# A hybrid decoder step: the state space scan in two halves, and one-operation softmax statistics

## The chip, the cores and the metric

The kernel runs on one core of a Trainium2 chip. The metric is the device time of one launch in microseconds (us); lower is better. The engines are PE (TensorE, matrix products), PEld (its weight loads), DVE (VectorE), ACT (ScalarE), POOL (GpSimd) and SP (SyncE, which here issues transfers). Each has its own instruction stream and runs it in order; semaphores tie the streams together.

## The reference

The program is one layer of a decoder with two branches, for 1024 prompt tokens and 64 new tokens (8 requests of 8). One projection of the normalised input gives the columns of both branches and of all gates. The S5 branch is a linear state space model: 64 groups of 16 channels, each with 64 complex states. The attention branch uses a compressed latent; the new tokens also attend to a paged cache of 4096 past tokens. Cut to what matters here:

```python
z = rmsnorm(x) @ w_in
u_s, g_s, cq, ckv_raw, kr_raw, g_a, m_s, m_a = split_in(z)
# S5 branch, by group g, state p, channel c
bu = einsum('gpc,blgc->blgp', b_bar, ug);  bu[:, 0] += lam_bar * h0
h  = associative_scan(lambda e1, e2: (e1[0]*e2[0], e2[0]*e1[1] + e2[1]), (lam_bar, bu), axis=1)
y  = real(einsum('gcp,blgp->blgc', c, h)) + d * u
y_s = (glu(gelu(y)) * silu(g_s)) @ w_br_ssm
# attention branch: prompt blocks of 128 queries, and pages with running max and sum
m_new = maximum(m, max(sp));  corr = exp(m - m_new);  pp = exp(sp - m_new)
l = l * corr + sum(pp);       acc = acc * corr + pp @ kc
y_a = (o * silu(g_a)) @ w_br_attn
h = x + (sigmoid(m_s) * y_s + sigmoid(m_a) * y_a) @ w_out;  y = rmsnorm(h)
```

## The kernel before

**Stripes.** A projection is computed in stripes of 128 output columns. For one stripe of the input projection PE runs 72 matmuls of 368 or 352 token columns (L152): each product is taken with a high and a low part of both factors. The 128x1024 weights of a stripe come in by SP (`wraw`), ACT casts them to `whi` (L94), and DVE or POOL subtracts to get `wlo` (L100). The stripes are called u, gs, ga, ms, ma by their columns; there are 8 of each.

**The S5 branch** works on blocks of 8 time steps. A *quarter* q is 16 groups, and has two halves h of 8 groups, so each u stripe feeds one half. For each half:

- `s5_inputs` builds the input matrices `Bm` on DVE (L545 to L547, 128x1024), turns them on PE (L553), multiplies them with u, which has been through memory (L561), and ACT copies the result into the state tile `S` (L566).
- `s5_consts` and `s5_toeplitz` build, on POOL, the output matrices `E` (L647 to L649, 128x1152) and the diagonal `dg` (L651), and on PE and ACT the matrix `Km` of the 8 steps in a block (L671 to L683).
- `s5_outputs` gathers the states into `Hg` (L693 on ACT, L694 on POOL), multiplies `Km` with u and `E` with `Hg` (L703, L705), and writes `Y` to memory.

`s5_scan` runs on DVE once for a quarter. The 136 block states are 16 runs of 8 and 8 new-token states. It has three parts: seven rounds of four 256-element operations that run along j, the position in a run (L586 to L589, stride of 8 elements in `S`); 16 steps of four 16-element operations that carry the run ends from run to run in a tile `R`; and a back substitution in 448-element operations (L616 to L619).

**Order.** Python generators issue work, and `woven` picks, at each turn, the stream with the least progress, so the weights of the streams set the order; `urgent`, `pin` and `PLAN` do the same for later stages:

```python
t = min(todo)
d = next(t[2])
t[0] += d / t[3]
...
for q in range(NQ):
    yield from self.woven((chain(q), 40), (self.s5_scan(q, sb), W3))
```

All eight u stripes come first, beside the S5 setup. Then `self.run((self.s5(sb, ps), 256), (fill(), W2))` weaves the S5 work with `fill`, which is 8 ms and 3 gs stripes. After it stand one gs stripe and one ga stripe, then the latents (q, k, v), the prompt attention and the decode attention. Both attentions are woven with "dense" stripes (the other gates, the output projections) by the numbers in `PLAN`, a list of (stripes, from, to) by attention steps. The names that the prediction uses are these: scan (L586 to L622), inputs (L545 to L566), consts (L647 to L651), outputs (L693 to L705), and the softmax lines L1007, L1014 (prompt), L1253, L1254, L1261 (decode).

Of the kernel before, what the change touches and what calls it, by code (L numbers as in the profile page):

```python
# [57 lines left out]
PLAN = ((6, MQ, MP - 1), (6, MP - 1, MP - 1), (3, MP + 2, MP + 14), (40, MP + 14, MD - 20), (2, MD - 18, MD - 1),  # L58
# [17 lines left out]
class Body:  # L76
# [211 lines left out]
    def stage_u(self, raws, outs, sb, ps):  # L288
        yield from self.stripes(self.a["w_in"], C_U, KT, (self.xh, self.xl), KT, raws, outs, ps, self.u_each(sb),
                                first=2)  # L290


    def s5_setup(self, sp, sb, ps):
# [93 lines left out]
        L4 = sp.tile([P, 4, G], F32, name="L4")  # L387
# [8 lines left out]
        tt = sp.tile([P, 2, G], F32, name="tt")  # L396
# [31 lines left out]
        sgn = sp.tile([P, 2], F32, name="sgn")  # L428
# [87 lines left out]
    def s5_inputs(self, q, sb, ps):  # L516

        nc = self.nc
        V = nc.vector
        S = sb.tile([P, PQ, 2, NCK + 1], F32, name="S", bufs=2)  # L520
        self.pin(V.memset(S[:, :, :, 0:1], 0.0), q == 0)
        self.S[q] = S
        for h in range(2):
            while self.u_done < 2 * q + h + 1:
                yield 0.5
            g0 = q * 2 * GB + h * GB
            gs = slice(g0, g0 + GB)
# [4 lines left out]
            U = sb.tile([P, GB, NCK], F32, name="UA")  # L532
# [4 lines left out]
            tb = sb.tile([P, GB, 8, GC], F32, name="tb")  # L537
# [31 lines left out]

    def s5_scan(self, q, sb):  # L570
# [35 lines left out]
        yield 0.8
        w1 = sb.tile([P, PQ // 2, NSUP, 7], F32, name="w1")
        w2 = sb.tile([P, PQ // 2, NSUP, 7], F32, name="w2")
        for a in (slice(0, PQ // 2), slice(PQ // 2, PQ)):
# [15 lines left out]
    def s5_consts(self, q, h, sb, ps):  # L625

        nc = self.nc
        Gp = nc.gpsimd
# [5 lines left out]
        for i in (nc.sync.dma_start(cb, self.bc_dram[0:2, :, gs].rearrange("i p g c -> p i g c")),
                  nc.sync.dma_start(Bz[:, :, GC:2 * GC], self.bc_dram[2, :, gs]),
                  nc.sync.dma_start(U, self.u_dram[:, gs])):
            if q == 0:
                self.behind(i, self.u_last)
# [16 lines left out]

    def s5_toeplitz(self, q, h, sb, ps):

        nc = self.nc
# [5 lines left out]
        for n in range(2):  # L664
            cols = slice(n * P, n * P + P)
            for x in range(3):
                for r in range(4):
                    g = 2 * r + n
                    o = b[r * W:(r + 1) * W, cols]
                    if x == 0:  # L670
                        i = nc.tensor.matmul(o, Bz[:, g, GC:], E[:, g, 1:9].rearrange("p t c -> p (t c)"), start=True, stop=False)  # L671
                        self.pin(i, r == 0)
                    elif x == 1:
                        nc.tensor.matmul(o, Bz[:, g, 0:W], E[:, g, 0:8].rearrange("p t c -> p (t c)"),
                                         start=False, stop=False)
# [1038 lines left out]
```

## Time and profile before

| | |
|---|---|
| median of 3 runs | 1879.74 us (1874.36 to 1880.57) |
| the profiled execution | 1876.06 us, span 1874.3 us, mean granted clock 0.972 |
| PE busy | 1726.3 us (92%) |
| DVE busy | 1232.0 us (66%) |
| ACT busy | 931.1 us (50%) |
| POOL busy | 784.5 us (42%) |

The page of the profile gives the busy time of each engine, and the span in 40 slices of 47 us. By the stages of the program the span reads: input and u stripes until 132 us; the S5 region from 132 to 406 us; one gs and one ga stripe until 430 us; latents until 755 us; prompt attention until 1200 us; decode attention until 1660 us; the last projections until 1874 us. In the slices, PE is at 9 tenths nearly everywhere, but at 6 to 8 tenths in slices 1 to 3 and in slices 4 to 8, the S5 region, where DVE is busiest.

### The profile page before, as it was taken

To read this page: it belongs to the slowest core of one execution; us is meant where nothing else is said; L and a number is where in the kernel's file an instruction comes from. 1 tells how busy PE (TensorE), PEld (TensorE's weight loads), DVE (VectorE), ACT (ScalarE), POOL (GpSimd) and SP (SyncE) were. 2 spreads that over 40 slices of the span, in tenths; PEclk is the share of its full clock that TensorE was granted. 3 is DMA by queue.
4 is the path that set the end of the run, shared out by engine and by line. 5 is a ranking of instruction groups with operands and counts; after the bars stand their busy time and mean duration, and the time that the engine had idled before them with its cause. 6 is when DMAs were issued, how large, how long until landed. Compare 5 with 4: busy or idle time off the path is not lost.

```text
span 1874.3 us, 32546 instructions
## 1 busy us (share of the span) xinstructions
PE 1726.3 (92%) x11434; PEld 1635.8 (87%) x11434; DVE 1232.0 (66%) x2847; ACT 931.1 (50%) x2269; POOL 784.5 (42%) x757
## 2 busy tenths in 40 slices
PE   6998866699998999999999899988999999999997
PEld 6998866699998988999999889887898899899997
DVE  7708999953334442788877888568787787644322
ACT  5226344432346443677766666455566566532222
POOL 2116334403455112665654545555455455322223
PEclk9999988899999999999999999999999999999999
DMA  8444334244456999565655753465555455275602
GB/s 204 139 99 141 103 92 114 53 129 126 122 172 211 326 311 295 132 183 156 188 146 146 202 138 87 153 232 182 177 179 177 162 164 178 85 248 147 192 9 96
DMA packets 263194, 299.60 MB, mean 160 GB/s; under 512 B 40272, under 2 KB 223288, under 8 KB 256760
## 3 DMA queue, kind: packets, MB, share of 16 engines
q1 hardware_dynamic: 234424, 231.97, 42.4%
q0 software_dynamic: 7872, 48.24, 7.5%
q10 hardware_dynamic: 20736, 17.31, 3.4%
q8 instruction: 91, 1.49, 0.3%
q14 instruction: 71, 0.58, 0.1%
HBM read 201.79 MB, written 95.66 MB: 159 GB/s over the span
## 4 chain that ended last, share of the span: by engine, by line
PE 59%; DVE 20%; DMA 9%; ACT 5%; issue 4%; POOL 2%; SPq 1%; ACTq 0%; POOLq 0%; DVEq 0%
PE mm L152 28%; PE sc L152 5%; PE sc L1000 4%; PE acc L1145 4%; PE tr L152 3%; PE tr L1035 3%; DVE sc L586 2%; DVE sc L588 2%; DVE S L589 2%; DMA ck<-cache_ckv,pidx 2%; DVE sc L587 2%; PE sc L1119 1%; PE acc L1049 1%; PE sc L1208 1%; PE acc L1048 1%
## 5 line engine op out<-in xcount | busy, mean ns | idle before, releaser
L152 PE MATMUL mm<-xT,whi 128*128 128x368 f32 (+1 forms) x1920 | 509.0, 339 | 14.2 <-DVE gst L775 13.8
L152 PEld LDWEIGHTS mm<-xT,whi 128*128 128x128 f32 x1920 | 346.0, 193 | 18.7 <-DVE gst L775 14.4
L152 PE MATMUL mm<-xT,wlo 128*128 128x368 f32 (+1 forms) x960 | 321.9, 336 | 0.0
L100 POOL TENSOR_TENSOR cl<-ck,ch 128x1024 fp32r<-128x1024 f32 x64 | 154.9, 2423 | 170.2 <-ACT ch L94 165.5
L152 PEld LDWEIGHTS mm<-xT,wlo 128*128 128x128 f32 x960 | 184.5, 192 | 1.3
L1016 POOL TENSOR_SCALAR p<-p,sm 128x1024 f32<-128x1024 f32 (+7 forms) x128 | 97.8, 768 | 123.4 <-DVE sm L1015 66.3
L94 ACT CAST pTh<-tr 128x256 fp32r<-128x256 f32 (+1 forms) x248 | 110.2, 451 | 68.4 <-PE tr L1035 53.3
L100 DVE TENSOR_TENSOR pTl<-tr,pTh 128x256 fp32r<-128x256 f32 (+1 forms) x248 | 125.9, 511 | 27.6 <-ACT pTh L94 18.2
L1000 PE MATMUL sc<-K,Q 128*128 128x384 f32 (+5 forms) x576 | 133.7, 347 | 5.9 <-ACT p L1011 5.8
L100 POOL TENSOR_TENSOR wlo<-wraw,whi 128x1024 fp32r<-128x1024 f32 x35 | 86.7, 2477 | 112.3 <-ACT whi L94 110.3
L1011 ACT ACTIVATE p<-sc,sm 128x320 f32<-128x320 f32 (+3 forms) x192 | 110.4, 581 | 35.8 <-DVE sm L1008 29.2
L1035 PE MATMUL tr<-ident,p 128*128 128x128 f32 x576 | 112.1, 275 | 9.9 <-DVE pTl L100 7.3
L1004 DVE TENSOR_REDUCE sm<-sc 128x1 f32<-128x128 f32 (+2 forms) x192 | 104.0, 550 | 12.3 <-PE sc L1000 8.4
L1000 PEld LDWEIGHTS sc<-K,Q 128*128 128x128 f32 x576 | 98.6, 191 | 12.8 <-ACT p L1011 8.4
L152 PE MATMUL mm<-z,whi 128*128 128x368 f32 (+1 forms) x384 | 108.2, 346 | 0.0
L152 PE MATMUL mm<-aT,whi 128*128 128x368 f32 (+1 forms) x384 | 107.7, 339 | 0.0
L94 ACT CAST whi<-wraw 128x1024 fp32r<-128x1024 f32 (+1 forms) x74 | 71.4, 965 | 69.9 <-PE mm L152 63.7
L152 PE MATMUL mm<-oT,whi 128*128 128x368 f32 (+1 forms) x384 | 95.3, 330 | 2.7 <-DVE gl L1409 2.7
L1035 PEld LDWEIGHTS tr<-ident,p 128*128 128x128 f32 x576 | 72.3, 141 | 18.6 <-issue 4.5
L1049 PE MATMUL acc<-pTl,Vt 128*128 128x256 f32 (+1 forms) x224 | 82.2, 367 | 1.3 <-DVE pTl L100 1.3
L94 ACT CAST ch<-ck 128x1024 fp32r<-128x1024 f32 x64 | 67.2, 1051 | 25.7 <-DMA ck<-cache_ckv,pidx 20.0
L1048 PE MATMUL acc<-pTh,Vt 128*128 128x256 f32 (+1 forms) x224 | 73.0, 326 | 2.2 <-DVE oT L1054 1.6
(486 smaller groups left out, 4746.4 us busy)
## 6 DMA issues: line engine op xcount, KB each, us to landing
wraw<-w_in SPq DMA_DIRECT2D x45, 512.0 KB, 5.0
krT<-kr_dram SPq DMA_DIRECT2D x64, 192.0 KB, 2.8
kr_dram<-krx SPq DMA_DIRECT2D x64, 128.0 KB, 2.6
v_dram<-vt SPq DMA_DIRECT2D x32, 256.0 KB, 4.3
Q<-qn_dram SPq DMA_DIRECT2D x32, 256.0 KB, 5.2
K<-kn_dram SPq DMA_DIRECT2D x32, 256.0 KB, 5.0
Vt<-v_dram SPq DMA_DIRECT2D x8, 1024.0 KB, 5.7
u_dram<-ust ACTq DMA_DIRECT2D x64, 68.0 KB, 3.6
```

What stands on the lines that cost most here:

```text
L94: nc.scalar.copy(hi, src)
L100: e.tensor_sub(lo, src, hi.bitcast(F32))
L152: i = nc.tensor.matmul(ps, row(s, k)[:, wsl], row(m, k)[(slice(None),) + xsl], start=start and k == j == 0, stop=stop and k == nk - 1 and ...
L586: V.tensor_mul(u1, src, qb(Q, k, n, True))
L1000: self.mark(nc.tensor.matmul(s[:, :w], qq[:, i * P:(i + 1) * P], kk[:, k0:k0 + w], start=j == 0, stop=j == 2), j == 0)
L1004: V.reduce_max(sm[:, x:x + 1], s[:, :w], axis=AX.X)
L1011: nc.scalar.activation(p[:, k0:k0 + w], s[:, :w], AF.Exp, bias=sm[:, 2:3], scale=SCALE, accum_out=sm[:, 3 + x:4 + x])
L1016: nc.gpsimd.tensor_scalar(p[:, :n], p[:, :n], sm[:, 5:6], 0.0, op0=ALU.mult, op1=ALU.add)
L1035: self.mark(nc.tensor.transpose(b[:, x * P:(x + 1) * P], ptl[x][:, k * P:(k + 1) * P], self.ident), x == s0)
L1048: self.mark(nc.tensor.matmul(po[:, o0:], w, th[:, o0:], start=k == 0, stop=False))
L1049: nc.tensor.matmul(po[:, o0:], w, tl[:, o0:], start=False, stop=k == nk - 1)
L1145: self.mark(nc.tensor.matmul(o[:, :KV], t[:kp, i * P:(i + 1) * P], pv(i)[x], start=j == 0 and i == 0, stop=j == 2 and i == nt - 1), i == 0)
```

## The change

The scan works on two halves of 32 groups (four *octets* of 8 groups each) where it worked on four quarters. The state tile is now `W[P, 16, 2, 9, 17]`: position in a run (9) outside and run (17) inside, so that an operation along j reads 16 neighbouring elements. The run carries stand in `W[..., 0, :]` and have no tile of their own. The rounds have 512 elements, the carry steps 32, the back substitution 420 in four pieces of 4 pairs. ACT's copies into `W` now scatter (read along k, write along j), and all four `Hg` copies are on ACT, reading `W` at a stride of 17 elements. `E`, `tm` and `dg` are built on DVE, and `wlo` stays on DVE in this region; both were POOL's.

The front of the program does six of the u stripes (0 to 5); stripes 6 and 7 begin `fill`, followed by 8 ms stripes and one gs stripe. The remaining gs stripes are woven with the outputs of the second half. Two ga stripes come before the latents (was one); `PLAN` has 37 stripes in its fourth entry (was 40), `NGA` is 3 (was 2).

In the softmax, maximum and scaling are one `tensor_scalar` (prompt: max then multiply; decode: multiply then min with the earlier negative maximum), and the two sums are `tensor_scalar`, too. `L4`, `tt` and `sgn` are moved to a scratch pool. The line numbers in the second half of each difference below are those of the new kernel; there, L100 is L102 and L152 is L154.

On POOL, at the place where the first outputs of the scan are made, the instructions before are these (names: `Hg` the gathered states, `E`, `tm`, `dg` and `wlo` as above):

```order
L694 TENSOR_SCALAR Hg<-S 64x4x136 x2
L647 TENSOR_TENSOR E_1412<-Pr,cb 128x8x144
L694 TENSOR_SCALAR Hg<-S 64x4x136 x2
L649 TENSOR_TENSOR E_1412<-E_1412,tm 128x8x144
L648 TENSOR_TENSOR tm<-Pi,cb 128x1152
L100 TENSOR_TENSOR wlo<-wraw,whi 128x1024
L647 TENSOR_TENSOR E_1413<-Pr,cb 128x8x144
L651 TENSOR_TENSOR dg<-dT,ident 32x256
```

Now POOL passes from the clearing of the S5 tiles straight to the gathering of the cached rope keys (`dkr`), which belongs to the stage after:

```order
L479 DMA bc_dram<-By 128x1024
L721 MEMSET Km_1224 128x1024
L722 MEMSET E_1226 128x8x16
L723 MEMSET Bz_1228 128x384
L721 MEMSET Km_1225 128x1024
L722 MEMSET E_1227 128x8x16
L723 MEMSET Bz_1229 128x384
L1177 DMA dkr<-cache_krope,pidx 128x256 x2
```

All of POOL's tensor work of the S5 region is gone from it.

On DVE, in a scan before, the carry steps have only the inputs of the next quarter (`Bm`) between them:

```order
L586 TENSOR_TENSOR sc_2090<-R,Q 128x16
L587 TENSOR_TENSOR sc_2091<-R,QS 128x16
L588 TENSOR_TENSOR sc_2090<-sc_2090,S 128x16
L589 TENSOR_TENSOR R<-sc_2090,sc_2091 128x16
L545 TENSOR_TENSOR Bm<-Pr,cbB 128x1024
L586 TENSOR_TENSOR sc_2090<-R,Q 128x16
```

Now DVE's stream holds consts and `wlo` as well. Here is the end of the first scan's back substitution (`w`), with the `E` of the third octet, which uses the tile of the first, and the first round of the second scan behind it:

```order
L622 TENSOR_TENSOR w_2261<-W,Q 128x420
L648 TENSOR_TENSOR E_1226<-Pr,cb 128x8x144
L624 TENSOR_TENSOR w_2261<-w_2261,w_2262 128x420
L102 TENSOR_TENSOR wlo<-wraw,whi 128x1024
L650 TENSOR_TENSOR E_1226<-E_1226,tm 128x8x144
L625 TENSOR_TENSOR W<-W,w_2261 128x4x7x15
L590 TENSOR_TENSOR sc_2313<-W,QS 128x512
```

What moved is that the second scan stands on DVE behind an `E` whose tile PE must first have read out. The core of the difference:

```diff
-PQ = GB
+OCT = 4
+PQ = OCT * PB
 NSUP = 16
-NGS = 3
-NGB, NGA = 1, 2
+NRUN = NSUP + 1
+NU = 6
+NGB, NGA = 2, 3
...
-PLAN = ((6, MQ, MP - 1), (6, MP - 1, MP - 1), (3, MP + 2, MP + 14), (40, MP + 14, MD - 20), (2, MD - 18, MD - 1),
+PLAN = ((6, MQ, MP - 1), (6, MP - 1, MP - 1), (3, MP + 2, MP + 14), (37, MP + 14, MD - 20), (2, MD - 18, MD - 1),
...
-        S = sb.tile([P, PQ, 2, NCK + 1], F32, name="S", bufs=2)
-        self.pin(V.memset(S[:, :, :, 0:1], 0.0), q == 0)
-        self.S[q] = S
-        for h in range(2):
...
+        W = sb.tile([P, PQ, 2, 9, NRUN], F32, name="W", bufs=2)
+        self.pin(V.memset(W[:, :, :, 0, 0:1], 0.0), q == 0)
+        self.W[q] = W
+        for o in range(OCT):
...
+            while self.u_done <= q * OCT + o:
+                yield 0.2
...
-                        nc.scalar.copy(S[e * 64:(e + 1) * 64, h * PB + n, x, 1:],
-                                       b[x * 64:(x + 1) * 64, e * NCK:(e + 1) * NCK])
+                        nc.scalar.copy(W[e * 64:(e + 1) * 64, o * PB + n, x, 1:9],
+                                       b[x * 64:(x + 1) * 64, e * NCK:(e + 1) * NCK].rearrange("p (k j) -> p j k", j=8))
...
-        for j in range(1, 8):
-            cmac(SPv[:, :, :, :, j], SPv[:, :, :, :, j - 1], SPv[:, :, :, :, j], 0, NSUP, t1, t2)
-            yield 1.0
-        R = sb.tile([P, PQ, 2, NSUP + 1], F32, name="R")
-        V.memset(R[:, :, :, 0:1], 0.0)
+        for j in range(2, 9):
+            cmac(W[:, :, :, j, 0:NSUP], W[:, :, :, j - 1, 0:NSUP], W[:, :, :, j, 0:NSUP], 0, NSUP)
+            yield 2.7
         for k in range(NSUP):
-            cmac(R[:, :, :, k + 1:k + 2], R[:, :, :, k:k + 1], SPv[:, :, :, k, 7:8], 7, 1, t1[:, :, :, 0:1], t2[:, :, :, 0:1])
+            dst = W[:, :, :, 0, k + 1:k + 2]
+            if k == NSUP - 1:
+                dst = self.hfin[:, :, 8, prs].rearrange("p x n -> p n x").unsqueeze(3)
+            cmac(dst, W[:, :, :, 0, k:k + 1], W[:, :, :, 8, k:k + 1], 7, 1)
...
+        n = PQ // 4
...
-                V.tensor_add(SPv[:, a, x, :, 0:7], SPv[:, a, x, :, 0:7], w1)
-                yield 1.5
-        V.tensor_copy(SPv[:, :, :, :, 7], R[:, :, :, 1:NSUP + 1])
-        V.tensor_copy(S[:, :, :, SEQ // 8:NCK], h0)
-        yield 1.0
...
+                V.tensor_add(W[:, a, x, 1:8, 1:NSUP], W[:, a, x, 1:8, 1:NSUP], w1)
+                yield 2.4
...
-        Gp.tensor_mul(E[:, :, 1:10], bp(self.Pr), bc(cb[:, 0]))
-        Gp.tensor_mul(tm, bp(self.Pi), bc(cb[:, 1]))
-        Gp.tensor_add(E[:, :, 1:10], E[:, :, 1:10], tm)
+        V.tensor_mul(E[:, :, 1:10], bp(self.Pr), bc(cb[:, 0]))
+        V.tensor_mul(tm, bp(self.Pi), bc(cb[:, 1]))
+        V.tensor_add(E[:, :, 1:10], E[:, :, 1:10], tm)
...
+        Hg = sb.tile([P, GB, NCK], F32, name="Hg", tag="Bm")
+        Hv = Hg.rearrange("p (n two) (k j) -> p n two k j", two=2, j=8)
         for x in range(2):
-            nc.scalar.copy(Hv[x * 64:(x + 1) * 64, :, 0], S[0:64, h * PB:(h + 1) * PB, x, 0:NCK])
-            nc.gpsimd.tensor_scalar(Hv[x * 64:(x + 1) * 64, :, 1], S[64:128, h * PB:(h + 1) * PB, x, 0:NCK],
-                                    1.0, 0.0, op0=ALU.mult, op1=ALU.add)
-        yield 2.0
-
-        Y = sb.tile([P, GB, NCK], F32, name="Y")
+            for e in range(2):
+                src = W[e * 64:(e + 1) * 64, o * PB:(o + 1) * PB, x, 0:8].rearrange("p n j k -> p n k j")
+                dst = Hv[x * 64:(x + 1) * 64, :, e]
+                nc.scalar.copy(dst, src)
...
+        self.W, self.U = {}, {}
         yield from self.s5_inputs(0, sb, ps)
-        for q in range(NQ):
-            yield from self.woven((chain(q), 40), (self.s5_scan(q, sb), W3))
-        yield from chain(NQ)
+        yield from self.woven((self.s5_scan(0, sb), 53), (self.s5_inputs(1, sb, ps), 22))
+        yield from self.woven((self.s5_scan(1, sb), 53), (self.s5_outs(0, sb, ps), 36))
+
+    def s5_outs(self, q, sb, ps):
+        for o in range(OCT):
+            yield from self.s5_consts(q, o, sb, ps)
+            yield from self.s5_toeplitz(q, o, sb, ps)
+            if o > 0:
+                yield from self.s5_outputs(q, o - 1, sb, ps)
+        yield from self.s5_outputs(q, OCT - 1, sb, ps)
...
-                V.tensor_max(sm[:, 0:1], sm[:, 0:1], sm[:, 1:2])
-            V.tensor_scalar(sm[:, 2:3], sm[:, 0:1], -SCALE, None, op0=ALU.mult)
+                V.tensor_scalar(sm[:, 2:3], sm[:, 0:1], sm[:, 1:2], -SCALE, op0=ALU.max, op1=ALU.mult)
+            else:
+                V.tensor_scalar(sm[:, 2:3], sm[:, 0:1], -SCALE, None, op0=ALU.mult)
...
             if len(parts) == 2:
-                V.tensor_add(sm[:, 3:4], sm[:, 3:4], sm[:, 4:5])
+                V.tensor_scalar(sm[:, 3:4], sm[:, 3:4], sm[:, 4:5], None, op0=ALU.add)
...
             if g >= 0:
-                V.tensor_max(nm[:, 0:1], nm[:, 0:1], d["m"])
-            V.tensor_scalar(nm[:, 1:2], nm[:, 0:1], -SCALE, None, op0=ALU.mult)
+                V.tensor_scalar(nm[:, 1:2], nm[:, 0:1], -SCALE, d["nm"], op0=ALU.mult, op1=ALU.min)
+            else:
+                V.tensor_scalar(nm[:, 1:2], nm[:, 0:1], -SCALE, None, op0=ALU.mult)
...
-                nc.scalar.activation(nm[:, 2:3], d["m"], AF.Exp, bias=nm[:, 1:2], scale=SCALE)
-                V.scalar_tensor_tensor(l, l, nm[:, 2:3], nm[:, 3:4], op0=ALU.mult, op1=ALU.add)
-            d["m"] = nm[:, 0:1]
+                nc.scalar.activation(nm[:, 2:3], d["nm"], AF.Exp, bias=nm[:, 1:2], scale=-1.0)
+                V.tensor_scalar(l, l, nm[:, 2:3], nm[:, 3:4], op0=ALU.mult, op1=ALU.add)
+            d["nm"] = nm[:, 1:2]
...
-                self.wlo = "pool"
 
                 def fill():
+                    yield from self.stage_u(wr, wo, gsb, ps, NU, KT)
                     yield from self.stage_gates(("ms",), wr, wo, gsb, ps)
-                    yield from self.stage_gates(("gs",), wr, wo, gsb, ps, n=NGS)
-                self.run((self.s5(sb, ps), 256), (fill(), W2))
+                    yield from self.stage_gates(("gs",), wr, wo, gsb, ps, n=1)
+                self.run((self.s5(sb, ps), 185), (fill(), 119))
+                self.run((self.s5_outs(1, sb, ps), 36),
+                         (self.stage_gates(("gs",), wr, wo, gsb, ps, first=1, n=4, pin=True), 33))
                 self.s5_states(sb, ps)
-                self.wlo = "dve"
-                self.run((self.stage_gates(("gs",), wr, wo, gsb, ps, first=NGS, n=4, pin=True), 1))
-                self.run((self.stage_gates(("ga",), wr, wo, gsb, ps, n=NGB, pin=True), 1))
+            self.run((self.stage_gates(("ga",), wr, wo, gsb, ps, n=NGB, pin=True), 1))
```

## Rows read from the trace of the kernel before

**Rows 1.** Busy time by stretch: us, PE, PEld, DVE, ACT, POOL busy, granted clock, DMA, GB/s
```profile
135.00:405.00 270.00, 209.91 (x1611) 200.28 (x1609) 247.86 (x509) 123.27 (x360) 113.89 (x56) 0.90 0.38 103
...
755.00:1200.00 445.00, 429.86 (x2699) 403.54 (x2698) 356.91 (x1050) 295.10 (x813) 242.25 (x301) 0.99 0.55 149
1200.00:1660.00 460.00, 433.30 (x2893) 396.86 (x2892) 338.82 (x638) 263.08 (x532) 220.48 (x126) 0.98 0.55 179
```

**Rows 2.** PE's waits, 135 to 405 us: total us, times, longest us
```profile
PE sc L553 <- DVE sc L588: 17.5, 2, 9.3
PE mm L152 <- DVE gst L775: 13.8, 3, 11.4
...
PE sc L703 <- ACT Km L683: 1.3, 1, 1.3
PE tr L705 <- ACT Hg L693: 0.4, 1, 0.4
```

**Rows 3.** Chain of waits in order of time: start us, us, what
```profile
80.82 51.10 PE mm L152 x311
...
406.21 15.87 PE mm L152 x96
```

**Rows 4.** DVE by line and shape, 130 to 405 us: busy us, mean ns | idle
```profile
L589 DVE TENSOR_TENSOR S<-sc,sc 128x256 f32<-128x256 f32 x28 | 33.7, 1205 | 0.7
...
L587 DVE TENSOR_TENSOR sc<-S,QS 128x256 f32<-128x256 f32 x28 | 27.0, 965 | 0.0
```

**Rows 5.** DVE timeline: start us, us, instruction
```profile
198.11 0.19 DVE L586 TENSOR_TENSOR sc<-R,Q 128x16 f32<-128x16 f32 x1
...
198.78 0.19 DVE L586 TENSOR_TENSOR sc<-R,Q 128x16 f32<-128x16 f32 x1
...
227.58 0.62 DVE L619 TENSOR_TENSOR S<-S,w 128x448 f32<-128x448 f32 x1
228.12 0.65 DVE L586 TENSOR_TENSOR sc<-S,Q 128x256 f32<-128x256 f32 x1
...
240.17 3.61 DVE L588 TENSOR_TENSOR sc<-sc,S 128x256 f32<-128x256 f32 x1
...
246.41 0.61 DVE L586 TENSOR_TENSOR sc<-S,Q 128x256 f32<-128x256 f32 x1
...
248.75 0.61 DVE L586 TENSOR_TENSOR sc<-S,Q 128x256 f32<-128x256 f32 x1
```

**Rows 6.** POOL timeline of the same place
```profile
240.63 2.67 POOL L649 TENSOR_TENSOR E<-E,tm 128x1152 f32<-128x1152 f32 x1
```

**Rows 7.** DVE by line and shape, whole run
```profile
L100 DVE TENSOR_TENSOR wlo<-wraw,whi 128x1024 fp32r<-128x1024 f32 x29 | 36.7, 1265 | 29.2 <-ACT whi L94 29.0
L100 DVE TENSOR_TENSOR pTl<-sc,pTh 128x512 fp32r<-128x512 f32 x40 | 27.3, 683 | 9.8 <-ACT pTh L94 9.0 <-PE acc L1145 0.9
```

**Rows 8.** PE timeline near the end of the scan
```profile
282.42 0.40 PE L703 MATMUL sc<-U,Km 128*128 128x136 f32 x2
282.65 0.40 PE L705 MATMUL sc<-Hg,E 128*128 128x136 f32 x2
...
294.46 0.42 PE L671 MATMUL sc<-E,Bz 128*32 128x128 f32 x8
...
296.00 0.66 PE L553 MATMUL tr<-ident,Bm 128*128 128x128 f32 x4
```

**Rows 9.** ACT by line and shape, whole run
```profile
L566 ACT COPY S<-sc 64x136 f32<-64x136 f32 x76 | 20.3, 267 | 6.3 <-PE sc L561 5.3
L772 ACT ACTIVATE gst<-mm 128x368 f32<-128x368 f32 x32 | 15.4, 480 | 14.8 <-PE mm L152 8.0 <-DMA u_dram<-ust 3.9 <-issue 2.7
...
L279 ACT COPY ust<-mm 128x368 f32<-128x368 f32 x16 | 13.8, 886 | 42.5 <-DMA u_dram<-ust 17.6 <-PE mm L152 13.3 <-issue 7.7
L693 ACT COPY Hg<-S 64x544 f32<-64x544 f32 x16 | 10.4, 650 | 29.7 <-DVE S L622 18.8 <-DVE S L619 5.8 <-DMA y_dram<-Y 5.0
```

**Rows 10.** Lines of the decode softmax: ns of one, min/median/max, start us
```profile
L1253 DVE TENSOR_TENSOR dnm<-dnm x64: 140/156/2795, 1234.1 to 1628.7; 128x1 f32<-128x1 f32 x64
...
L1254 DVE TENSOR_SCALAR dnm<-dnm x72: 135/153/155, 1233.5 to 1628.9; 128x1 f32<-128x1 f32 x72
```

**Rows 11.** PE's waits, 1200 to 1660 us
```profile
PE acc L1145 <- DVE dacc L1279: 6.3, 3, 4.9
...
PE tr L1208 <- DVE dnm L1254: 2.4, 3, 0.9
```

More of the change, by code (lines that the diff above doesn't have):

```diff
@@ L286, in u_each, with stage_u @@
         return each
-    def stage_u(self, raws, outs, sb, ps):
-        yield from self.stripes(self.a["w_in"], C_U, KT, (self.xh, self.xl), KT, raws, outs, ps, self.u_each(sb),
-                                first=2)
+    def stage_u(self, raws, outs, sb, ps, first, n):
+        yield from self.stripes(self.a["w_in"], C_U, n, (self.xh, self.xl), KT, raws, outs, ps, self.u_each(sb),
+                                first=first)
     def s5_setup(self, sp, sb, ps):
@@ L386, in s5_setup @@
             self.pin(i, q == 0)
-        L4 = sp.tile([P, 4, G], F32, name="L4")
+        L4 = sb.tile([P, 4, G], F32, name="L4", bufs=1)
         V.tensor_copy(L4.rearrange("p q g -> p (q g)"), b[:, :4 * G])
@@ L395, in s5_setup @@
         V.tensor_copy(Pi[:, 1], L4[:, 1])
-        tt = sp.tile([P, 2, G], F32, name="tt")
+        tt = sb.tile([P, 2, G], F32, name="tt", bufs=1)
         def cmul(dr, di, ar, ai, br, bi, n):
@@ L426, in s5_setup @@
         self.Q, self.QS = Q, QS
-        sgn = sp.tile([P, 2], F32, name="sgn")
+        sgn = sb.tile([P, 2], F32, name="sgn", bufs=1)
         nc.gpsimd.memset(sgn[0:64, 0:1], 1.0)
@@ L531, in s5_inputs @@
                 self.behind(i, self.u_last)
[L532 removed]
+            while self.u_done <= q * OCT + o:
+                yield 0.2
+            U = sb.tile([P, GB, NCK], F32, name="UA", tag="U", bufs=2)
             i = nc.sync.dma_start(U, self.u_dram[:, gs])
@@ L536, in s5_inputs @@
             Bm = sb.tile([P, GB, 8, GC], F32, name="Bm")
-            tb = sb.tile([P, GB, 8, GC], F32, name="tb")
+            tb = sb.tile([P, GB, 8, GC], F32, name="tb", tag="tm")
             def bp(t):
@@ L605, in s5_scan @@
             V.tensor_copy(self.hfin[:, x, 0:8, prs].rearrange("p b n -> p n b"), smp[:, :, x])
[L606 to L609, printed above, removed]
+        V.tensor_copy(W[:, :, :, 0:8, NSUP], h0)
+        yield 3.0
+        n = PQ // 4
+        for a in range(0, PQ, n):
+            a = slice(a, a + n)
+            w1 = sb.tile([P, n, 7, NSUP - 1], F32, name="w1", tag="sc1")
+            w2 = sb.tile([P, n, 7, NSUP - 1], F32, name="w2", tag="sc2")
@@ L618, in s5_scan, with s5_consts @@
                 V.tensor_add(w1, w1, w2)
-                V.tensor_add(SPv[:, a, x, :, 0:7], SPv[:, a, x, :, 0:7], w1)
-                yield 1.5
-        V.tensor_copy(SPv[:, :, :, :, 7], R[:, :, :, 1:NSUP + 1])
-        V.tensor_copy(S[:, :, :, SEQ // 8:NCK], h0)
-        yield 1.0
-    def s5_consts(self, q, h, sb, ps):
+                V.tensor_add(W[:, a, x, 1:8, 1:NSUP], W[:, a, x, 1:8, 1:NSUP], w1)
+                yield 2.4
+    def s5_consts(self, q, o, sb, ps):
         nc = self.nc
-        Gp = nc.gpsimd
-        g0 = q * 2 * GB + h * GB
+        V = nc.vector
+        g0 = (q * OCT + o) * GB
         gs = slice(g0, g0 + GB)
-        cb = sb.tile([P, 2, GB, GC], F32, name="cb")
-        E, Bz, Km = self.Es[h], self.Bz[h], self.Kms[h]
+        cb = sb.tile([P, 2, GB, GC], F32, name="cb", bufs=2)
+        E, Bz = self.Es[o % 2], self.Bz[o % 2]
         U = sb.tile([P, GB, NCK], F32, name="U", bufs=2)
[L634 to L638, printed above, removed]
+        nc.sync.dma_start(cb, self.bc_dram[0:2, :, gs].rearrange("i p g c -> p i g c"))
+        nc.sync.dma_start(Bz[:, :, GC:2 * GC], self.bc_dram[2, :, gs])
+        nc.sync.dma_start(U, self.u_dram[:, gs])
         tm = sb.tile([P, GB, 9, GC], F32, name="tm")
@@ L1539, in front @@
                         yield from self.stage_x(xT, wr, wo, gsb, self.pool(s3, "xs", 2, side=R), ps)
-                    yield from self.stage_u(wr, wo, gsb, ps)
+                    yield from self.stage_u(wr, wo, gsb, ps, 2, NU)
                 with ExitStack() as s3:
```

83 lines of the change are left out of this document (33 added, 50 removed).

## The prediction

> **What bounds the kernel now.** I read the span by stages first, then for each stage what PE waits for, then the engine that PE waits for. In the two attention stages PE is busy 429.86 of 445 us and 433.30 of 460 us [rows 1]: work taken off DVE there can give back at most the remainders, 15 and 27 us. The S5 region differs. In 270 us PE is busy 209.91, at a granted clock of 0.90, while DVE is busy 247.86 [rows 1]. Ten lines of PE's waits, from 17.5 us on DVE's L588 to 0.4 us on ACT's `Hg`, add up to 59 us [rows 2]. DVE sets the pace there.
>
> What that costs follows from PE's own work. 311 stripe matmuls take 51.10 us, 0.1643 us each, so a stripe of 72 is 11.83 us [rows 3]. The S5 products come at 0.116 us each (two pairs of them start at 282.42 and 282.65), and one set of E products takes 1.54 us (294.46 to 296.00) [rows 8]. The region has 384 of the first, 44.5 us; eight sets at some 1.4 us, 11; and the transposes, 8: in sum 63.5 us. When the S5 work is over, at 406.21, the chain has a run of 96 stripe matmuls [rows 3], of which the first 72 are the last gs stripe, which thus ends at 418. From the end of u at 132 us until then there are 12 stripes, 142 us. With the 63.5 us PE could be done at 337.5; the trace has 418, so the region loses 80.5 us. No edit to it can return more.
>
> Why is DVE so slow? A round of four 256-element operations starts at 246.41 and the next at 248.75: 2.34 us, 0.585 each [rows 5]. Yet the means of L589 and L587 are 1205 and 965 ns [rows 4]. The DVE operation that starts at 240.17 takes 3.61 us and ends at 243.78 [rows 5]; POOL's E operation lasts from 240.63 to 243.30 [rows 6]. So a DVE operation with both inputs in SBUF lasts as long as POOL's where they overlap. The 112 operations of the rounds use 121 us, by these means; at 0.585 they would use 65.5.
>
> **The change part by part.**
>
> *DVE in the S5 region.* Removed: the stretching by POOL, whose order is empty there. Rounds: 56 operations of 512 elements. A 512-element DVE subtraction with one input in PSUM takes 683 ns, a 1024-element one from SBUF 1265 [rows 7], half of which is 0.63. I take 0.68: 38 us. Bounds are 0.62 and, if the slowness is not POOL's, twice the present means, 1.93 to 2.41 (a rival, below). Carry: 32 steps instead of 64, of 32 elements; a step of 16 takes 0.67 (198.11 to 198.78) [rows 5], I take 0.73: 23.5 us. Back substitution: 64 operations of 420 elements, where one of 448 starts 0.54 before the next [rows 5]: 34.6. Inputs, 24 at 1.27 [rows 7]: 30.5. Added from POOL: 24 E operations of 1152 elements at 1.40 (the 1265 ns by size), 33.6; `dg`, 8 at some 0.43, 3.4; `wlo`, 14 at 1.27, 17.8. Gate evictions and the rest: 12. In sum 194 us, against 247.86 now, although 55 us of it were POOL's.
>
> *The scan's new layout.* The rounds read 16 neighbours where they read at 32 bytes. The price of the stride on DVE is small or none by the rows: the strided 256 elements take 0.61 when not stretched, the 448 in runs of seven 0.62 [rows 5], so up to 0.25 us of an operation may be the stride's. The 0.68 holds half of that.
>
> *When the scan can start and end.* Six u stripes end at 37.5 + 71 = 108.5 us instead of 132 (37.5 is 132 less eight stripes). In PE's order the products of the first half's inputs end at stripe 8.8: 37.5 + 104 + 7.5 us of S5 products = 149, and ACT's last 16 copies of 0.267 [rows 9] make it 153 to 155. DVE has done some 20 of its 194 us by then (twelve inputs, four `wlo`), so 174 remain: 329 without idle time. One idle place can be read from the order: the third octet's E stands behind PE's first outputs, and the second scan behind that E. The first piece of the first scan is done 61 us after its start, at 216 (rounds 19, carry 12, inputs and `wlo` 21, E 6, back substitution 3). ACT needs 11.6 us for `Hg` and `Km`, so outputs begin at 228 where PE's order is at 224, and the E waits 4 to 8 us. The second half's third E, behind which some 10 us of DVE's work stand, is thus done at 323 to 329. PE has then 1.33 stripes to do, 15.7 us, three outputs of 32 products, 11.1, and two E sets, 3: 30 in all. So the gs stripes end at 353 to 359 if DVE is never held up otherwise. Today DVE is idle 22 of the 270 us [rows 1]; a third of that, 7 us, I add: 363 instead of 418, **55 us**, bounds 40 (15 us more of idle time) and 80.5.
>
> *ACT.* All `Hg` copies are on ACT, 32 instead of 16, and strided; the copies into `W` scatter. The rows bound this: ACT's strided `ust` write takes 886 ns where a plain one of its size takes 480 [rows 9], 1.85 times. By that a copy into `W` costs up to 0.49 instead of 0.267 (128 of them, 29 us at most) and an `Hg` copy 1.2 instead of 0.65. ACT is busy 123 of 270 us [rows 1], so this lies beside the scan except at two places: the 16 copies ahead of the first scan, +3.6 at most, and the four `Hg` copies ahead of an output, +2.2. The 7 us of idle time hold half of these.
>
> Against the `Hg` layout speaks the Trainium skill ("SBUF — State Buffer", the box on 16-byte cachelines in the section "Door 1: The DMA port swizzle"): each access that crosses to a new line pays, which at 68 bytes every element does. The 886 ns of `ust` agree. By the rule every `Hg` copy is at its upper end, and the sum loses some 2 us.
>
> *The ga stripe and PLAN.* One stripe of 11.83 us goes from the prompt attention to ahead of the latents. PE is 97% busy in the prompt [rows 1], so that stage gets shorter by nearly as much; where the stripe filled a wait it is lost. 0 to 11.8 us, I take 2. There is no gain in it, as PE's work is the same.
>
> *Softmax.* 64 operations of L1253 go, of up to 2795 ns; the `tensor_scalar` beside it is never over 155 [rows 10]. L1261, L1007 and L1014 lose a second tensor input in the same way. What PE gets back are its waits on DVE's L1279 (6.3) and L1254 (2.4) in decode [rows 11]: **I take 9**. Bounds are 0 and the 42 us of both remainders; nothing is added, so no loss.
>
> The skill has a rule against this, too (same page, section "Who interferes with whom"): `tensor_scalar` can enter modes that also contend with GpSimd. L1254's maximum of 155 ns, with POOL half busy, says that a one-element one does not. By the rule the 9 us would be 0 and the sum 1827.
>
> *The sum.* 1876.06 - 55 - 9 + 2 = 1814 for the profiled execution; the median lies 3.7 us above it, so **1818 us**.
>
> **The rivals.**
>
> *The chain binds harder.* DVE has next to no idle time from 155 to 330, and each `gst` eviction, E and `wlo` stands in its order; PE already waits 13.8 us for evictions [rows 2]. If these waits stay and ACT's copies are at their upper ends, some 28 of the 55 us go: 1846. Against it: DVE has less work in sum.
>
> *PE-bound.* If 512 elements take 0.62 and the weave leaves few waits, 72 us of the 80.5 come, and 15 from softmax: 1880 + 2 - 72 - 15 = 1795. Against it: the scan still starts at 153.
>
> *Slower.* The means of L587 and L589 may belong to the operations, not to POOL. Then the 512-element ones take some 2.2 us instead of 0.68, 85 us more on a chain that nothing covers; the gs stripes end at 448, 30 us late, and the time is 1880 + 30 - 9 + 2 = 1903. It decides from 1.8 us each, where 56 times the excess eats 55 + 9 - 2 = 62 us. Against it: the round of 2.34 us.
>
> *No effect.* If the transfers of u and of its matrices set the region, it stays within 0.3% of 1880. PE's waits name no transfer [rows 2].
>
> **How the numbers follow.** Forecast 0.72, its own range 1800 to 1838 (S5 40 to 65, softmax 0 to 15, ga 0 to 12). Harder chain 0.14, PE-bound 0.06, slower 0.05, none 0.03. A difference under 0.3%, 5.6 us, can't be told from no change. The range reaches to the PE-bound case below and past the harder chain above, 1790 to 1856. Faster is 0.72 + 0.14 + 0.06 = 0.92, same 0.03, slower 0.05.
>
> **What would show it.** DVE's 512-element operations near 0.68 us, the maximum close to the mean; no tensor work on POOL between 95 and 340 us; DVE busy some 194 us in the region; PE's waits there 10 to 20 us instead of 59; first outputs at 228, the gs stripes done at 363. In decode no one-element operation of DVE over 0.3 us. The forecast is wrong if the rounds' operations take over 1.2 us, if an `Hg` copy takes over 2 us, or if PE waits as long for evictions and E as it now does for the scan.

## The result and the profile after

The changed kernel takes 1808.78 us (median of 4 runs, 1804.02 to 1810.31), the kernel before 1877.05 (4 runs): a ratio of 0.9633, interval 0.9602 to 0.9664. The forecast was 1818, its range 1790 to 1856. The profiled execution took 1809.99 us, with a span of 1808.2, 66.1 us shorter than before.

Busy time by stretch of the changed kernel, columns as in [rows 1]; the first is the S5 region:

```profile
108.00:357.00 249.00, 236.37 (x1840) 229.05 (x1839) 181.71 (x345) 162.20 (x392) 0.00 (x0) 0.97 0.45 125
700.00:1122.00 422.00, 404.20 (x2508) 376.26 (x2507) 334.39 (x973) 285.28 (x798) 234.19 (x299) 0.98 0.58 155
1122.00:1570.00 448.00, 430.14 (x2845) 395.38 (x2844) 295.64 (x586) 268.29 (x534) 227.93 (x132) 0.99 0.54 175
```

PE is busy 95% of the S5 region, where it was 78%, at a granted clock of 0.97 instead of 0.90 [rows 1]; POOL does nothing. PE's waits from 100 to 360 us are all here, 12.7 us instead of 59 [rows 2]:

```profile
PE sc L678 <- DVE dg L652: 9.1, 1, 9.1
PE tr L707 <- ACT Hg L697: 2.3, 2, 2.0
PE sc L705 <- ACT Km L684: 1.3, 1, 1.3
```

DVE by line and shape, 100 to 405 us. The rounds of the scan are L589 to L592, as L586 to L589 in [rows 4]:

```profile
L648 DVE TENSOR_TENSOR E<-Pr,cb 128x1152 f32<-128x1152 f32 x8 | 10.8, 1356 | 8.1 <-PE sc L707 7.3 <-PE tr L707 0.6
...
L592 DVE TENSOR_TENSOR W<-sc,sc 128x512 f32<-128x512 f32 x14 | 9.7, 690 | 0.2
...
L625 DVE TENSOR_TENSOR W<-W,w 128x420 f32<-128x420 f32 x16 | 9.5, 594 | 0.4
...
L592 DVE TENSOR_TENSOR W<-sc,sc 128x32 f32<-128x32 f32 x30 | 6.7, 223 | 0.9
```

An operation of 512 elements takes 690 ns on the mean, where one of 256 took 1205. ACT in the S5 region, to compare with [rows 9]:

```profile
L697 ACT COPY Hg<-W 64x544 f32<-64x544 f32 x32 | 37.2, 1164 | 0.4
L569 ACT COPY W<-sc 64x136 f32<-64x136 f32 x76 | 20.3, 267 | 7.6 <-PE sc L564 3.9 <-DMA u_dram<-ust 2.7
```

The marks along DVE, PE and ACT (timelines) give the first operation of the scan, the first product with a gathered state, the third octet's E, and the last `Y` copy, with which PE has done all gs stripes and all S5 products:

```profile
155.07 0.69 DVE L589 TENSOR_TENSOR sc<-W,Q 128x512 f32<-128x512 f32 x1 [4.00 <-ACT W L569]
```
```profile
227.84 0.50 PE L707 MATMUL tr<-Hg,E 128*128 128x136 f32 x2 [2.05 <-ACT Hg L697]
```
```profile
235.22 1.36 DVE L648 TENSOR_TENSOR E<-Pr,cb 128x1152 f32<-128x1152 f32 x1 [5.40 <-PE sc L707]
```
```profile
357.28 0.42 ACT L708 COPY Y<-tr 128x272 f32<-128x272 f32 x1
```

**The ledger by stage**, from the same marks in both traces: the end of PE's gs and S5 work (418.0, now 357.1), first and last row maximum of the prompt (748.9 and 1176.1, now 702.4 and 1121.0), first and last of the decode (1232.9 and 1628.0, now 1178.8 and 1562.5), and the span.

| stage | before | now | difference |
|---|---|---|---|
| until gs stripes and S5 outputs are done | 418.0 | 357.1 | -60.9 |
| ga stripe(s) and latents | 330.9 | 345.3 | +14.4 |
| prompt attention | 427.2 | 418.6 | -8.6 |
| between | 56.8 | 57.8 | +1.0 |
| decode attention | 395.1 | 383.7 | -11.4 |
| the rest | 246.3 | 245.7 | -0.6 |

### The profile page after: what moved, and what is told of

It is laid out like the page before. It is cut to its first block, busy times and chain, and to the rows that moved or that the text cites. A ratio compares the mean times of both kernels' runs of the same rounds, so it can differ in the third digit from the quotient of the medians.

```text
span 1808.2 us, 32219 instructions
## 1 busy us (share of the span) xinstructions
PE 1712.5 (95%) x11434; PEld 1624.7 (90%) x11434; DVE 1101.1 (61%) x2551; ACT 959.9 (53%) x2285; POOL 662.5 (37%) x697
## 4 chain that ended last, share of the span: by engine, by line
PE 71%; DMA 10%; DVE 6%; ACT 5%; issue 3%; POOL 2%; SPq 1%; ACTq 0%; POOLq 0%; DVEq 0%
PE mm L154 35%; PE sc L154 5%; PE sc L995 4%; PE acc L1141 4%; PE tr L154 3%; PE tr L1031 3%; DMA ck<-cache_ckv,pidx 2%; PE acc L1044 2%; PE acc L1045 2%; PE sc L1115 2%; PE sc L1204 2%; PE tr L1115 1%; PE tr L1204 1%; DMA v_dram<-vt 1%; PE sc L1127 1%
## 5 line engine op out<-in xcount | busy, mean ns | idle before, releaser
L154 PE MATMUL mm<-xT,whi 128*128 128x368 f32 (+1 forms) x1920 | 502.4, 336 | 0.4 <-ACT xT L230 0.4
L154 PEld LDWEIGHTS mm<-xT,whi 128*128 128x128 f32 x1920 | 340.2, 190 | 4.5 <-ACT xT L230 0.5
L154 PE MATMUL mm<-xT,wlo 128*128 128x368 f32 (+1 forms) x960 | 319.7, 333 | 0.0
L102 POOL TENSOR_TENSOR cl<-ck,ch 128x1024 fp32r<-128x1024 f32 x64 | 156.9, 2452 | 167.3 <-ACT ch L96 148.4
L154 PEld LDWEIGHTS mm<-xT,wlo 128*128 128x128 f32 x960 | 182.3, 190 | 0.8
L102 DVE TENSOR_TENSOR pTl<-tr,pTh 128x256 fp32r<-128x256 f32 (+1 forms) x248 | 126.1, 512 | 38.6 <-ACT pTh L96 22.2
L1177 POOL DMA_INDIRECT dkr<-cache_krope,pidx x32 | 34.0, 1063 | 285.4 <-DMA wraw<-w_in 278.1
L1012 POOL TENSOR_SCALAR p<-p,sm 128x128 f32<-128x128 f32 (+7 forms) x128 | 97.7, 766 | 92.4 <-DVE sm L1011 45.0
L1007 ACT ACTIVATE p<-sc,sm 128x128 f32<-128x128 f32 (+2 forms) x192 | 110.8, 583 | 30.4 <-DVE sm L1002 15.0
L995 PEld LDWEIGHTS sc<-K,Q 128*128 128x128 f32 x576 | 97.9, 190 | 16.4 <-ACT p L1007 11.4
L999 DVE TENSOR_REDUCE sm<-sc 128x1 f32<-128x128 f32 (+3 forms) x192 | 103.3, 550 | 11.8 <-PE sc L995 8.7
L154 PE MATMUL mm<-z,whi 128*128 128x368 f32 (+1 forms) x384 | 109.7, 347 | 0.0
L154 PE MATMUL mm<-aT,whi 128*128 128x368 f32 (+1 forms) x384 | 106.9, 337 | 0.0
L154 PE MATMUL mm<-oT,whi 128*128 128x368 f32 (+1 forms) x384 | 95.5, 331 | 3.4 <-DVE gl L1407 3.4
L102 DVE TENSOR_TENSOR wlo<-wraw,whi 128x1024 fp32r<-128x1024 f32 (+1 forms) x53 | 61.7, 1164 | 53.3 <-ACT whi L96 47.8
```

The source lines that it names most:

```text
L102: e.tensor_sub(lo, src, hi.bitcast(F32))
L154: i = nc.tensor.matmul(ps, row(s, k)[:, wsl], row(m, k)[(slice(None),) + xsl], start=start and k == j == 0, stop=stop and k == nk - 1 and ...
L995: self.mark(nc.tensor.matmul(s[:, :w], qq[:, i * P:(i + 1) * P], kk[:, k0:k0 + w], start=j == 0, stop=j == 2), j == 0)
L999: V.reduce_max(sm[:, x:x + 1], s[:, :w], axis=AX.X)
L1007: nc.scalar.activation(p[:, k0:k0 + w], s[:, :w], AF.Exp, bias=sm[:, 2:3], scale=SCALE, accum_out=sm[:, 3 + x:4 + x])
L1012: nc.gpsimd.tensor_scalar(p[:, :n], p[:, :n], sm[:, 5:6], 0.0, op0=ALU.mult, op1=ALU.add)
```

## The experiments

The changed kernel was run again beside the later ones:

> The changed kernel as it is, for comparison with the others of this call: 1804 to 1812.

It gave 1807.61 us (5 runs; ratio to before 0.9642, 0.9619 to 0.9664). Differences in groups 1 and 2 are to 1808.78, in 3 and 4 to 1807.61.

**1. What freed the scan.** Two kernels take one part out of the change, a third puts one into the kernel before.

*E, tm, dg and wlo on POOL again, in the changed kernel:*

```diff
-        V.tensor_mul(E[:, :, 1:10], bp(self.Pr), bc(cb[:, 0]))
+        Gp.tensor_mul(E[:, :, 1:10], bp(self.Pr), bc(cb[:, 0]))
...
+                self.wlo = "pool"
```

> The changed kernel with E, tm, dg on POOL again and wlo of the S5 region on POOL again; the scan in two halves and everything else stay. Theory (POOL's tensor work stretches DVE operations with two SBUF inputs, and this is what the region lost): the means of the scan's 512-element operations rise from 0.69 us to 1.0 to 1.6, with maxima over 2.5, DVE is busy longer although 55 us of work have left it, the gs stripes end 20 to 35 us after 357, time 1829 to 1845. Rival (the new layout and the larger operations made the scan fast, and DVE only gained work): 512-element means stay at 0.69, time 1809 or, with 55 us less on DVE, down to 1795.

Measured: 1833.9 us, ratio 0.9768 (0.9739 to 0.9797); the last `Y` copy starts at 385.0. DVE and POOL by line, 100 to 385 us:

```profile
L592 DVE TENSOR_TENSOR W<-sc,sc 128x512 f32<-128x512 f32 x14 | 20.2, 1442 | 0.4
```
```profile
L649 POOL TENSOR_TENSOR E<-Pr,cb 128x1152 f32<-128x1152 f32 x8 | 23.0, 2880 | 42.5 <-PE sc L708 27.1 <-DMA cb<-bc_dram 15.3
```

In the same layout and order of the scan, the same 512 elements take 1442 ns instead of 690 on L592, and 982 to 1144 instead of 685 to 688 on the three other lines of a round. The theory holds, and with it the reason why work was worth moving onto the engine that sets the pace: 25 us.

*All eight u stripes ahead of the scan:*

```diff
-NU = 6
+NU = 8
...
-                    yield from self.stage_u(wr, wo, gsb, ps, NU, KT)
```

> The changed kernel with all eight u stripes ahead of the scan, the fill without them. Theory (DVE's chain sets the end of the region, so its start counts): first scan starts some 20 to 24 us later, gs stripes end 15 to 24 us later than 357, time 1824 to 1833. Rival (PE's work sets the end now): same work on PE, end and time unchanged within 4 us, 1805 to 1813.

Measured: 1833.99 us, 0.9768 (0.9744 to 0.9791). The first operation of the scan starts at 178.97 instead of 155.07, the last `Y` copy at 380.6 instead of 357.3: 23.9 us late at the start, 23.3 at the end, 25 in the time. DVE's chain sets the end from its first operation on.

*The kernel before with those four on DVE:*

> The kernel before with E, tm, dg and the wlo of the S5 region on DVE, nothing else changed: four quarters, old layout, eight u stripes first. Theory (both causes are needed: DVE without POOL's stretch but with four scans of small strided operations and 55 us more work has no less to do): 256-element means fall to 0.6 us with maxima near the mean, DVE busy in the region about 240 as before, time 1862 to 1882. Rival (POOL's stretch was the whole loss): time 1820 to 1840.

Measured: 1854.69 us, 0.9885 (0.9858 to 0.9912), the last `Y` copy at 385.4 instead of 405.9. DVE, 130 to 400 us:

```profile
L589 DVE TENSOR_TENSOR S<-sc,sc 128x256 f32<-128x256 f32 x28 | 17.8, 634 | 0.4
```

The stretch is gone in the old layout, too (1205 to 634), and that alone is worth 20.5 us of the 60.9. The time lies between my 1862 to 1882 and the rival's 1820 to 1840; neither holds. If the parts add, the start's 23 us leave some 17 for the scan in two halves with its new tile, its other order and `Hg` off POOL; this remainder wasn't tried by itself. One part of it can be read. In the changed kernel, DVE, 100 to 405 us, two operations of 256 elements differ in their inputs: the first reads `W` at 68 bytes, the second its input `h` in runs of 8 neighbours.

```profile
L591 DVE TENSOR_TENSOR sc<-sc,W 128x256 f32<-128x256 f32 x2 | 1.2, 610 | 0.0
...
L589 DVE TENSOR_TENSOR sc<-h,Q 128x256 f32<-128x256 f32 x2 | 0.8, 425 | 0.1
```

The old rounds, strided at 32 bytes, took 628 to 714 ns for 256 elements without POOL's stretch, so by estimate some 0.2 us of each was the stride's. The rounds of the whole region use DVE 73 us there (112 operations) and 38.5 in the changed kernel (56 operations).

**2. The ga stripe.**

```diff
-NGB, NGA = 2, 3
+NGB, NGA = 1, 2
-PLAN = ((6, MQ, MP - 1), (6, MP - 1, MP - 1), (3, MP + 2, MP + 14), (37, MP + 14, MD - 20), (2, MD - 18, MD - 1),
+PLAN = ((6, MQ, MP - 1), (6, MP - 1, MP - 1), (3, MP + 2, MP + 14), (40, MP + 14, MD - 20), (2, MD - 18, MD - 1),
```

> The changed kernel with one ga stripe before the latents as it was, and PLAN's 40 (NGB 1, NGA 2). Theory (the moved stripe costs 15.0 us ahead of the latents and the prompt gets only 9 back): 1800 to 1806. Rival (the prompt attention gives back the full 11.8): 1807 to 1811. Second rival (the prompt is better off with fewer stripes): above 1811.

Measured: 1817.93 us, 0.9675 (0.9651 to 0.9699), 9 us slower than the changed kernel. Its prompt, first to last maximum, is 4.3 us longer (422.9 us), although it holds a stripe of 11.8 us more, and PE's longest wait, from 340 to 700 us, is a new one:

```profile
PE mm L154 <- ACT wwhi L96: 12.1, 1, 12.1
```

It is for the first weights of the latents, whose load stands on SP behind the states' transfers after the scan. The second ga stripe is what PE does meanwhile; in the changed kernel that wait is 2.3 us. From the last `Y` copy to the first maximum of the prompt it is 346.6 us without the stripe and 345.1 with it, so there the stripe costs nothing. In the kernel before, two stripes stood at this place as well, the last gs and one ga; the change weaves the gs into the outputs, and the second ga takes its place. My theory of the run was wrong by its sign. The time is the second rival's.

**3. The softmax.**

*Decode as before, and decode with as many operations as in the change but two tensor inputs:*

```diff
-                V.tensor_scalar(nm[:, 1:2], nm[:, 0:1], -SCALE, d["nm"], op0=ALU.mult, op1=ALU.min)
+                V.scalar_tensor_tensor(nm[:, 1:2], nm[:, 0:1], -SCALE, d["nm"], op0=ALU.mult, op1=ALU.min)
```

> The changed kernel with the decode softmax as before (tensor_max, then scaling; the running sum with scalar_tensor_tensor). Theory (one-element operations with two tensor inputs are stretched by POOL there, on the path to the exponentials, and the decode stage got 11.8 us shorter by their removal): the tensor_max has maxima over 2 us again, the stage is 8 to 14 us longer, time 1817 to 1823. Rival (the decode stage got shorter because of what stands ahead of it, its place against POOL's work): within 4 us of the changed kernel.

> The changed kernel with scalar_tensor_tensor for the decode maximum and sum: as many operations, two tensor inputs. Theory (second tensor input): about as the old lines there, 1816 to 1823. Rival (the additional operation): 1804 to 1812.

Measured: 1822.22 us (0.9710, 0.9687 to 0.9733) and 1820.26 (0.9702, 0.9673 to 0.9731), 14.6 and 12.7 us slower. The line that gives the negative maximum, min/median/max ns, in the changed kernel run again and in the second variant:

```profile
L1250 DVE TENSOR_SCALAR dnm<-dnm x64: 195/206/215, 1180.9 to 1560.6; 128x1 f32<-128x1 f32 x64
...
  ACT dp L1257: 16.8, 19
```
```profile
L1250 DVE SCALAR_TENSOR_TENSOR dnm<-dnm x64: 144/160/2368, 1172.5 to 1569.7; 128x1 f32<-128x1 f32 x64
...
  ACT dp L1257: 49.0, 35
```

One operation either way, and shorter at the median with two tensors; but its longest is 2368 ns, and the exponential waits 49 us for it instead of 17. So it isn't the number of operations that costs. What differs is the second tensor input, and with it the order: some 300 of PE's 11,434 matmuls stand elsewhere than in the changed kernel, which no run held fixed. The stage as a whole speaks for the input. From first to last maximum it lasts 395.1 to 398.0 us in the five traces with two-tensor lines, the kernel before and two of its variants among them, and 380.2 to 385.5 in the nine with the new lines, whatever their order.

*The same pair for the prompt, and the new prompt lines alone in the kernel before:*

> The changed kernel with the prompt softmax as before (64 tensor_max and 64 tensor_add of one element). Theory (the same stretch, but PE is 97% busy and 15 us is all that the stage can lose): 2 to 6 us longer, 1811 to 1815. Rival (hidden altogether): within 2 us of the changed kernel, and DVE's busy time higher without effect.

> The changed kernel with as many operations in the prompt softmax, but with two tensor inputs each: max and scaling by scalar_tensor_tensor with a constant tile, the sum by tensor_add. Theory (it is the second tensor input, stretched while POOL works, that costs the prompt 24 us when the old lines stand there): maxima of 1.5 us and more, the prompt 10 to 20 us longer, 1818 to 1828. Rival (the number of operations, or the order that follows from it): within 5 us of the changed kernel, 1803 to 1813.

> The kernel before with the new prompt softmax alone. Theory (the new lines are worth by themselves what the old ones cost in the changed kernel): 8 to 22 us faster than before, 1854 to 1868. Rival (the old lines cost that much only beside the changed kernel's order of stripes): within 5 us of before.

Measured: 1831.98 us (0.9771, 0.9749 to 0.9793), 24 us slower; 1811.66 (0.9652, 0.9624 to 0.9679), 4 slower; and 1874.16 (0.9979, 0.9963 to 0.9995), 3.5 faster than before, with an interval that all but reaches 1. The first lies outside both of its expectations, in the other two the rival came true. The prompt lasts 438.4 us with the old lines. PE's waits there, 700 to 1150 us, and the two-tensor line of the second kernel:

```profile
PE tr L1030 <- DVE pTl L102: 12.5, 13, 2.8
PE sc L995 <- ACT p L1006: 7.4, 7, 2.9
```
```profile
L1004 DVE SCALAR_TENSOR_TENSOR sm<-sm,nsc x64: 201/216/2502, 705.6 to 1126.0; 128x1 f32<-128x1 f32 x64
```

Here the operations are stretched as in the decode, to 2502 ns, and it costs only 4 us in all. In this trace the prompt lasts 427.0 us, 8 more than the 418.6 of the changed kernel, and the stage ahead of it is 4 shorter. So of the 20 us by which the old lines make the prompt longer, the second tensor input explains 8 at most. What is left is the additional operations or the order: with the old lines some 430 of PE's 11,434 matmuls stand elsewhere, with the two-tensor ones some 290. In the order of the kernel before the same lines are worth 3.5 us. Which of the two it is stays open.

**4. Two attempts at a faster version.**

*dg on POOL:*

```diff
-        V.tensor_mul(dg, self.dT[:, gs].unsqueeze(2).to_broadcast([2 * GC, GB, 2 * GC]),
+        nc.gpsimd.tensor_mul(dg, self.dT[:, gs].unsqueeze(2).to_broadcast([2 * GC, GB, 2 * GC]),
```

> The changed kernel with only the eight dg products (32x256) on POOL. PE's one long wait in the region is 9.1 us on a dg that stands on DVE behind the carry steps. Theory (that wait delays Km, the first outputs and the E that waits for them): the wait goes, Hg of the first octet ends near 222 instead of 228, the gs stripes end 4 to 6 us earlier, time 1802 to 1805. Rival (PE then waits for Hg by as much, the scan being what is late): within 2 us of the changed kernel. Second rival (POOL's products stretch the carry steps): 0 to 4 us longer.

Measured: 1801.2 us (1798.86 to 1804.61), ratio 0.9601 (0.9578 to 0.9624), 6.4 us faster. The wait for dg is gone, another of 5.2 us for ACT's `Km` shows in its place:

```profile
PE sc L672 <- ACT Km L684: 5.2, 1, 5.2
PE tr L707 <- ACT Hg L697: 2.1, 1, 2.1
```

The last `Y` copy is at 355.7, where the changed kernel has 357.3 and, run again, 360.0. In the six traces with the changed kernel's S5 region (these two, and the four with old or two-tensor softmax lines) it lies between 356.2 and 361.6, so the 6.4 us can't be found in this mark. The first `Hg` product is at 228.64, where the same two traces have 227.84 and 230.19: the scan was late, too, as the first rival said. PE's waits in the region fall from 12.7 to 9.7 us only. The time lies just below the theory's 1802 to 1805, but its path through an earlier `Hg` isn't shown, and where most of the gain arises stays open. The second rival's stretch exists on a small scale: L623 (`w`, 420 elements) has a mean of 642 ns instead of 587.

*On top of it, Hg, the products and U in the order of W:*

```diff
-        Hv = Hg.rearrange("p (n two) (k j) -> p n two k j", two=2, j=8)
+        Hv = Hg.rearrange("p (n two) (j k) -> p n two j k", two=2, j=8)
...
-                i = nc.tensor.matmul(t, Km[:, g], U[:, g], start=True, stop=False)
+                i = nc.tensor.matmul(t, Km[:, g], U[:, g].rearrange("p (k j) -> p j k", j=8), start=True, stop=False)
```

> The changed kernel with dg on POOL, and with Hg, the state products and the U operand in the order of W: ACT copies without a stride, PE reads U at 32 bytes, ACT reads PSUM at a stride when it takes Y out. Theory (ACT's stride of 68 bytes is what makes an Hg copy 1.16 us, and four of them stand ahead of the first outputs): a copy takes 0.65, the first outputs come 2 us earlier, 1796 to 1801. Rival (the stride moves its price to PE or to the Y copies): U products over 0.15 us each or Y copies over 0.6, 1801 or more.

Measured: 1815.86 us (0.9678, 0.9645 to 0.9710), 14.7 us slower than with dg on POOL alone, all else in the same order; the six runs spread from 1807.83 to 1822.73. The last `Y` copy is at 365.6 instead of 355.7, so 9.9 us are lost in the region. ACT's copy and PE's products with U, first here, then in the kernel with dg on POOL:

```profile
L697 ACT COPY Hg<-W 64x544 f32<-64x544 f32 x32 | 20.7, 648 | 2.2 <-DVE W L625 1.8
```
```profile
L705 PE MATMUL tr<-U,Km 128*128 128x136 f32 x64 | 21.0, 418 | 0.0
```
```profile
L705 PE MATMUL tr<-U,Km 128*128 128x136 f32 x64 | 12.9, 284 | 0.0
```

ACT's copy falls from 1164 to 648 ns, 16.5 us in all, and PE pays for it with U at 32 bytes. The rival holds. The price of a stride moves to the engine that reads at it; ACT had time for it, PE hadn't.

## Why the prediction was right, point by point

- *DVE is freed by taking POOL's work away.* Right, and shown from both sides (690 against 1442 ns, 634 against 1205). The 512-element operations took 0.69 (forecast 0.68), the pieces of 420 0.59, E 1.356 (1.40). DVE is busy 181.7 us from 108 to 357; the sum of 194 was 12 too high.
- *The layout.* "Small or none" was a wrong reading of the stride's price on DVE: 610 ns strided against 425 in runs of 8, for 256 elements. The bound beside it, 0.25 us, holds it.
- *The marks.* Scan from 155 (forecast 153 to 155), first `Hg` product at 227.8 (228), E's wait 5.4 us (4 to 8). The E ahead of the second scan was started at 235.2.
- *The size of the S5 gain.* 60.9 where the sum has 55. Two terms were mis-sized, and their errors cancel in part. The second half's third E is done at 326.65, inside the 323 to 329 forecast for it (by the sum's own terms, 329 + 4 to 8 - 10, that is 323 to 327). But from 155 until then DVE is busy 151.2 us where 174 - 10 = 164 were summed, and idle 20.5 where the waits for E with the added "a third of that, 7 us" make 11 to 15. So DVE's work was put 13 too high and its idle time 5 to 9 too low, and the 363 came out 6 late; that the 353 to 359 without the 7 hold the measured 357 is partly luck. Of the idle time 5.4 us stand at the place that the order shows, the rest in pieces of under 2 us, most of them before `wlo` and gate evictions for which ACT was late.
- *ACT.* `Hg` at 1164 ns was at the upper end (1.2), a price taken from `ust`. By the Trainium skill's rule on 16-byte cachelines ("SBUF — State Buffer", section "Door 1: The DMA port swizzle") every one of these copies pays, and the trace agrees: 1164 at 68 bytes, 648 without a stride. The copies into `W` stayed at 267, at the lower end, though they read PSUM at 32 bytes.
- *The ga stripe.* "There is no gain in it, as PE's work is the same" was wrong as a bound: the stripe covers a wait of 12.1 us for the latents' weights, and without it the kernel is 9 us slower. Against the kernel before, though, this stage and the prompt together got 5.8 us longer (+14.4 - 8.6), with the prompt softmax's gain in it, where I had 2. I had priced the stripe against the prompt alone, not against what PE does between the scan and the latents. The -60.9 and the +14.4 belong together, as the gs stripe that left this stage counts in both: by the first maximum of the prompt the gain is 46.4 us, where 55 less a stripe of 11.8 makes 43.
- *Softmax.* 9 forecast; the decode gave 11.4 by the ledger and 14.6 by undoing it. The Trainium skill's rule that `tensor_scalar` can contend with GpSimd when its operands meet certain conditions ("SBUF — State Buffer", section "Who interferes with whom"), if it held for one element, would have made it 0; the longest of L1250 is 215 ns. The prompt had no share set apart. Its stage lasts 427.2 us before, 423.9 with the new lines alone, 422.9 in the changed kernel without the moved stripe, and 418.6 with it: by these single traces, 3.3 of the 8.6 us are the new lines' and 4.3 the stripe's. Undone in the changed kernel the same lines cost 24.
- *The 9.2 us between forecast and median.* By the ledger, 5.9 are S5's; the stages behind it gave 5.2 us where 9 - 2 = 7 were forecast, 1.8 the other way. The other 5 are the step from one execution to the median: 3.7 us were added for it, and the changed kernel's profiled run lies 1.2 above its median. The 1838 that ends the forecast's own range isn't the sum of its three bounds, which is 1880 - 40 + 12 = 1852.

## What to carry to other kernels

When an operation's mean is far above its undisturbed time, look on the other engines' timelines for what it coincides with before counting its elements: moving 55 us of work onto the busiest engine freed it here. Prefer operations with one tensor input on a path where POOL works in parallel: in the decode that was worth 11 to 15 us, in the prompt by itself some 3. Price a moved piece of work by the wait that it covers at its new place, not only by what it leaves.

## What was not expected of the hardware

ACT reads PSUM at a stride of 32 bytes at no price (267 ns before and after), but SBUF at 68 bytes at 1.8 times (1164 to 648 ns). PE's moving operand at 32 bytes costs, too: 418 ns on the mean instead of 284. DVE pays for strides as well: 610 ns against 425 for 256 elements. And a one-element DVE operation with two tensor inputs took up to 2502 ns here, 2795 before.
